# Four moves in the order of an encoder block's kernel: an earlier load for the second MLP operand, weight blocks that join later, two spacings changed

## The chip, the cores and the metric

The kernel runs on one core of a Trainium2 chip. The metric is the device time of one execution in microseconds, lower is better, as the median of several executions.

## The reference

One layer of a bidirectional encoder, for 1024 tokens of width 1024 in float32:

```
u = rms_norm(x);  q,k,v,cB,cC,cH,gA,gB = split(u @ w_in)
y_A = neighbourhood_attention(rms_norm(q), rms_norm(k), v) @ w_attn_branch
y_B = (cB * conv3(cC * cH)) @ w_conv_branch
m   = sigmoid(gA) * y_A + sigmoid(gB) * y_B
x   = x + m @ w_o
x   = x + relu(rms_norm(x) @ w_mlp_in)^2 @ w_mlp_out
```

The MLP's inner width is 4096.

## The kernel before, in words

The engines are named as in the profile: PE (TensorE, matmuls), DVE (VectorE), ACT (ScalarE), POOL (GpSimd) and SP (SyncE, whose queue issues every load, store and DMA transpose). Each engine works through its own instructions in the order in which the program issued them; an instruction that waits holds up all that stand behind it on its engine.

**Numbers.** Every float32 operand is scaled by a power of two and split into two float16 parts, high and low (ACT makes the high part by a scaled copy, DVE the low part by a multiply and subtract). A product is three passes over those parts (high by high, high by low, low by high). The scale of a weight block needs the block's largest value or sum of squares over all partitions. DVE reduces along each partition (L301 and L309 for a `Chunk`, L924 for the `forms_sum` blocks), writes a column (`ones_col`, L311 or L925), and PE adds it up with a 128 x 128 matmul of ones (`all_sum`, L179). These one-column matmuls stand in PE's stream like any other product.

**Seven products for eight.** The gates (S), the MLP's first product (W1) and its second (W2) are made with a 2 x 2 block scheme that needs seven block products. Its inputs are sums and differences of blocks ("forms"); its outputs are put together from the seven products by DVE. For a gate group or a W1 group `seven` issues seven units of twelve matmuls; each unit takes a PSUM bank in turn (`anybank`, eight banks under the names d, s and o).

**What orders the work.** The instructions' order is set when the program is built, by a hand-written schedule. `unit` issues the matmuls of one unit, then calls `step` and `tick` a given number of times. `step` advances every generator of the list `fg` (work that follows from products), `tick` advances the first generator of the list `bg` (preparation of later weights). A generator that yields is continued at a later tick. `apart` makes a generator wait until so many units, or so many matmul columns (`work`), have been issued. `built` and `need` drive the background list by force until a block is ready. `load_upto` issues the next weight loads on SP when an earlier block has been split and its buffer is free (five `raw` buffers in turn).

**Stages around the change.**
- *Gate groups*, n = 0 to 7. At the start of group n the preparation of S for n+1 (`prep_s`) is put on the background list, and for n = 1, 3, 5 that of the next A and B blocks (the projections of the attention and convolution branches, `Chunk.prep`). Then the group's products (`gate_units`), then those with A and B (`branch_units`), which `built` makes wait for the blocks. `turn_s` issues DMA transposes of the activations on SP.
- *Output projection* (`proj`, lines 1217 to 1248): 16 units of 24 matmuls with the blocks O0 and O1. O1's preparation is put on the background list ahead of them. After the units of the second half, `pair(n)` normalises two row blocks, makes the forms (L1138), splits them (L1163 on ACT, L1165 on DVE) and issues two DMA transposes (L1169) into u2T and u2x, the activations of the MLP's first product. `pair` makes a form only when the transposes of the pair before it have been issued, and issues those only when W1's group 0 is ready.
- *MLP, first product*: 16 groups q (`quad`), each with its W1 block (`sums1`, `prep1`). DVE's posts (L1295, L1298, L1299, L1300, L1303, L1308, L1310) put the products together and free their banks; `h_done` then squares (L1269, L1271), adds on POOL (L1138) and stores the forms of h to DRAM (L1275). Each store holds four groups' parts of one quarter s.
- *MLP, second product*: 28 operands, seven for each quarter, numbered 16 to 43. `prep2` makes one: ACT and DVE split the h form (L1384, L1386), then the weight (L1389, L1393). Its buffer becomes free when the products of group or operand i-2 are issued (`gate`). Operand 16 uses w11, 17 the form t2, made by POOL (L1399, L1400) after operand 16's splits. The load of h for operand 16 is issued by `first2`, for operand 17 inside the loop (L1377), for 18 and on by `h_load` (L1343).

Of the kernel before, what the change touches and what calls it, by code (L numbers as in the profile page):

```python
# [10 lines left out]
F32 = mybir.dt.float32  # L11
F16 = mybir.dt.float16
# [40 lines left out]
def encoder_block(ctx: ExitStack, tc: tile.TileContext, x, weights, cols, gqk, rel, masks, out):  # L53
# [106 lines left out]
    def apart(mark, n=3, of=units):  # L160
        while of[0] < mark + n and not forced[0]:
            yield WAIT
# [57 lines left out]
    class Chunk:  # L220
# [75 lines left out]
        def largest(self, rm, a, b):  # L296
            o = 0
            for p, (k, w) in enumerate(self.widths):
                while len(self.raw) <= p:
                    yield WAIT  # L300
                V.tensor_reduce(sc[:, at(rm, o, k)], self.raw[p][:, :k * w].rearrange("p (k w) -> p k w", k=k),  # L301
                                axis=AX, op=OP.max, apply_absolute_value=True)
                o += k
                yield
            while not self.ready:
                yield WAIT
            mul(rm, self.rows, rm)
            yield
            V.tensor_reduce(sc[:, a], sc[:, rm], axis=AX, op=OP.max, apply_absolute_value=True)  # L309
            c = ones_col()  # L310
            V.tensor_copy(c, sc[:, a])  # L311
            if self.kind != "V":
                yield from apart(units[0], {"A": 3, "B": 3, "O": 1}[self.kind])
            yield from all_sum(c, b, bank(self.bank) if self.bank else anybank(), 1e-30, self.kind != "V")

    def push(*chunks):
        for ch in chunks:
            bg.append(ch.prep())
# [602 lines left out]
    def sum_of(sm):  # L921

        b, a = cols_of("prep", 1), ones_col()
        V.tensor_reduce(sc[:, b], sc[:, sm], axis=AX, op=OP.add)  # L924
        V.tensor_copy(a, sc[:, b])  # L925
        return a, work[0]
# [136 lines left out]
    for n in range(8):  # L1063
        built(cG if n == 0 else cS[n])
        if n < 7:
            bg.append(prep_s(n + 1))
        if n in (1, 3, 5):
            push(cA[n // 2 + 1], cB[n // 2 + 1])
        m = w3p.tile([128, 2, 512], F32, name="m", bufs=1)
        mf = m.rearrange("p a t -> p (a t)")  # L1070
        if n < 7:
            sg = gate_units(n)
            if n == 0:
                turn_s(0, 2)

            def post(g, half, ps, iv, sg=sg, m=m):
                t = sg[:, 2 * half + g]
                V.scalar_tensor_tensor(t, ps, iv, t, op0=OP.mult, op1=OP.mult)
                if g == 1:
                    V.tensor_tensor(m[:, half], sg[:, 2 * half], t, op=OP.add)  # L1080
            branch_units(n, post)
            late.append(lambda n=n, mf=mf: fg.append(m_done(n, mf)))
        else:
            push(cO[0])
            tick(4)
            y = w3p.tile([128, 4, 512], F32, name="gsum", bufs=1)
            branch_units(n, lambda g, half, ps, iv: A.activation(y[:, 2 * half + g], ps, AF.Copy, scale=iv))
            settle()
            drain()
            s7 = tmp()  # L1090

            def bound():
                mm, m2, mx = tmp(4), tmp(2), tmp()
                V.tensor_reduce(sc[:, mm], y, axis=AX, op=OP.max, apply_absolute_value=True)
                yield
                V.tensor_tensor(sc[:, m2], sc[:, mm.start:mm.start + 4:2], sc[:, mm.start + 1:mm.start + 4:2],
                                op=OP.add)
                V.tensor_reduce(sc[:, mx], sc[:, m2], axis=AX, op=OP.max)
                yield from pow2(mx, 14, s7, at(rowsM, 7))
                for ch in cO:  # L1100
                    ch.ready = True

            fg.append(bound())

            def last(sg, half):
                o = slice(2 * half, 2 * half + 2)
                V.tensor_tensor(sg[:, o], sg[:, o], y[:, o], op=OP.mult)
                V.tensor_tensor(m[:, half], sg[:, 2 * half], sg[:, 2 * half + 1], op=OP.add)
                t = slice(512 * half, 512 * half + 512)
                A.activation(M[0][:, 7, t], m[:, half], AF.Copy, scale=sc[:, s7])  # L1110
                V.scalar_tensor_tensor(M[1][:, 7, t], m[:, half], sc[:, s7], M[0][:, 7, t],
                                       op0=OP.mult, op1=OP.subtract)

            gate_units(7, last)
            X1 = base.tile([128, 8, D], F32, name="x1", tag="Q")
            for b in range(8):
                SP.dma_start(X1[:, b], x[b * 128:(b + 1) * 128, :])
            settle()
# [73 lines left out]
    def sums1(q):  # L1192

        ch = c1[q]
        while q == 2 and pair_done[0] < 4:
            yield
        if q == 0:
            tsum[0] = U2[1][:, 2].rearrange("p s k t -> p (s k t)").bitcast(F32).rearrange("p (i c) -> p i c", i=4)
        elif q % 2:
            t = wsp.tile([128, 2, 4, 512], F32, name="tsum", tag="ws")  # L1200
            for i in range(2):
                tsum[q + i] = t[:, i]
        yield from rows_scaled(ch, g2)
        yield from forms_sum(ch, tsum[q], 3 if q > 1 else 2)

    def prep1(q):

# [13 lines left out]
    def proj(b, half, post=None, mms=None):  # L1221
        ps = anybank()

        def fin():
            o = X1[:, b, 512 * half:512 * half + 512]
            V.scalar_tensor_tensor(o, ps, sc[:, cO[half].inv], o, op0=OP.mult, op1=OP.add)
            if post:
                post()
        mm = tok_mms(ps, actM, b, cO[half], 8, 512, 0)
        if mms is None:  # L1230
            unit(mm, fin, 6, 4)
        else:
            mms.append((mm, fin))

# [112 lines left out]
    def prep2(s):  # L1347
# [11 lines left out]
        for i in range(2):  # L1359
            A.activation(j, x2[:, 2 * i:2 * i + 2].rearrange("p a c -> p (a c)"), AF.Square, scale=sc[:, iR],  # L1360
                         accum_out=sc[:, at(sm, 4 + i)])
            yield
        sw, inv = yield from scale_of(sum_of(sm), 0)
        fw = keep()
        mul(iR, sw, fw)
        c2[s].inv = inv
# [2 lines left out]
        for o, (f, name) in enumerate(ORDER):  # L1369
            n = 7 * s + o  # L1370
            i = 16 + n
            yield from gate(i)
            pool, tag = TAGS[i % 3]
            P = OPS[i] = pool.tile([128, 2, 2, 2048], F16, name="ops", tag=tag)
            if n == 1:
                later["h", 1] = P[:, 0].rearrange("p w m -> p (w m)").bitcast(F32).rearrange("p (k t) -> p k t", k=4)
                SP.dma_start(later["h", 1], HS[0][:, ORDER[1][0]])  # L1377
                yield from wait(8)
            while ("h", n) not in later:
                yield  # L1380
            if 1 < n < 26:
                h_load(n + 2)
            hf = later.pop(("h", n)).rearrange("p k t -> p (k t)")
            A.activation(P[:, 1, 0], hf, AF.Copy, scale=sc[:, Rs])  # L1384
            yield
            V.scalar_tensor_tensor(P[:, 1, 1], hf, sc[:, Rs], P[:, 1, 0], op0=OP.mult, op1=OP.subtract)  # L1386
            w = {"w11": w11, "t1": w11, "t3": w12, "w21": w21, "w22": w22}.get(name) or [T2[:, i] for i in range(2)]
            for i2 in range(2):
                A.activation(P[:, 0, 0, 1024 * i2:1024 * i2 + 1024], w[i2], AF.Copy, scale=sc[:, fw])  # L1389
            yield  # L1390
            for i2 in range(2):
                sl = slice(1024 * i2, 1024 * i2 + 1024)
                V.scalar_tensor_tensor(P[:, 0, 1, sl], w[i2], sc[:, fw], P[:, 0, 0, sl], op0=OP.mult, op1=OP.subtract)  # L1393
                yield
            ready.add(i)
            if name == "w11":
                T2 = later["t2"]()
                for i2 in range(2):
                    G.tensor_tensor(w11[i2], w11[i2], w12[i2], op=OP.add)  # L1399
                    G.tensor_tensor(T2[:, i2], w11[i2], w22[i2], op=OP.add)  # L1400
                    yield
            elif name == "t2":
                for i2 in range(2):
                    G.tensor_tensor(w12[i2], w12[i2], w22[i2], op=OP.add)
                yield
            elif name == "t3":
                for i2 in range(2):
                    G.tensor_tensor(T2[:, i2], T2[:, i2], w21[i2], op=OP.add)
                yield
            elif name == "t1":  # L1410
                done[0] += 4
                load_upto(done[0] + 5)
                if s < 3:
                    w2x_load(s + 1)
                    bg.append(prep2(s + 1))
            yield
# [146 lines left out]
```

## Time and profile before

| | |
|---|---|
| median of 3 runs | 1305.25 us (1305.03 to 1309.44) |
| the profiled execution | 1304.02 us, of which the span 1302.2 |
| mean granted TensorE clock in it | 0.979 |
| PE busy | 1220.6 us, 6294 matmuls |
| DVE busy | 933.8 us, 1719 instructions |
| ACT busy | 763.3 us, 1169 |
| POOL busy | 436.5 us, 269 |
| DMA | 173.35 MB, mean 133 GB/s |

Times in the text are microseconds from the start of the span of this execution. In a line of the timeline the columns are start, duration, engine, line, operation, output<-input and shape, and how many alike follow each other; in brackets stands the idle time of the engine before it and what ended it. A window's line gives its length, the busy time of PE, PEld, DVE, ACT and POOL with their counts, then the granted clock, the DMA share and GB/s. Ends of matmuls are modelled: a 128x512 matmul has 0.38 as its own, while one starts every 0.216 at full clock.

### The profile page before, as it was taken

How to read it: one execution, taken by the hardware profiler on the slowest of the kernel's cores; microseconds unless marked ns; L12 is line 12 of the kernel's file. 1: busy time of each engine (PE TensorE's matmuls, PEld its weight loads, DVE VectorE, ACT ScalarE, POOL GpSimd, SP SyncE). 2: the span in 40 equal slices, each digit the busy share in tenths (PEclk: the TensorE clock that was granted, in tenths of full speed). 3: DMA queues.
4: the chain of work that ended last, by engine and by line, in shares of the span. 5: the costliest groups of instructions: out<-in, count | busy, mean ns of one | idle time of the engine just before them, and what ended most of it. 6: DMA issues, size and time to landing. Idle time of an engine off the chain costs nothing.

```text
span 1302.2 us, 17008 instructions
## 1 busy us (share of the span) xinstructions
PE 1220.6 (94%) x6294; PEld 580.2 (45%) x6294; DVE 933.8 (72%) x1719; ACT 763.3 (59%) x1169; POOL 436.5 (34%) x269
## 2 busy tenths in 40 slices
PE   4999998888998999999997899999997799999998
PEld 3444444444443444444456444444443344444443
DVE  6578767878648776776575476667744588889798
ACT  6777567667454444524665678777773564646530
POOL 2430010121220211101022576667735516080562
PEclk9999998999999999999998999999998899999999
DMA  6558435646552121325284443445453662626112
GB/s 249 125 194 160 108 68 122 131 89 130 118 117 87 48 65 33 84 65 208 53 163 109 146 168 133 160 162 178 161 203 121 221 255 83 241 98 242 65 65 97
DMA packets 170803, 173.35 MB, mean 133 GB/s; under 512 B 131424, under 2 KB 131936, under 8 KB 166624
## 3 DMA queue, kind: packets, MB, share of 16 engines
q1 hardware_dynamic: 170720, 172.27, 44.8%
q8 instruction: 49, 0.80, 0.2%
q14 instruction: 34, 0.28, 0.1%
HBM read 102.51 MB, written 37.75 MB: 108 GB/s over the span
## 4 chain that ended last, share of the span: by engine, by line
PE 61%; DVE 13%; issue 8%; ACT 7%; DMA 7%; POOL 4%; SPq 1%; DVEq 0%; POOLq 0%; ACTq 0%
PE ps_d L188 22%; PE ps_s L188 19%; PE ps_o L188 13%; PE ps_d L854 4%; DVE w_ws L278 1%; DMA PT<-P 1%; DMA u2x<-v 1%; POOL as L1138 1%; DMA xt<-in_x 1%; DVE ops L1393 1%; DVE P L818 1%; DVE sz L792 1%; ACT w L977 1%; POOL sform L480 1%; DMA hf<-hs 1%
## 5 line engine op out<-in xcount | busy, mean ns | idle before, releaser
L188 PEld LDWEIGHTS <-w 128*128 128x128 f16 x1512 | 149.4, 100 | 160.4 <-issue 9.4
L188 PEld LDWEIGHTS <-ops 128*128 128x128 f16 x1356 | 133.1, 98 | 182.7 <-issue 21.2
L1138 POOL TENSOR_TENSOR as<-as 128x512 f32<-128x512 f32 x64 | 111.7, 1745 | 95.2 <-ACT as L1271 91.4
L188 PE MATMUL ps_s<-ops 128*128 128x512 f16 (+1 forms) x528 | 123.1, 384 | 17.6 <-ACT ops L1389 7.0
L854 PE MATMUL ps_d<-uT,w_ws 128*128 128x512 f16 x528 | 129.1, 386 | 2.4 <-ACT w_ws L290 2.4
L188 PE MATMUL ps_d<-ops 128*128 128x512 f16 x492 | 112.9, 379 | 0.0
L188 PEld LDWEIGHTS <-uT 128*128 128x128 f16 x648 | 64.4, 100 | 70.4 <-issue 6.8
L1384 ACT ACTIVATE ops<-hf,sc 128x2048 f16<-128x2048 f32 x26 | 51.9, 1994 | 70.4 <-PE ps_d L188 24.6
L188 PE MATMUL ps_d<-u2T,w 128*128 128x512 f16 (+1 forms) x420 | 90.1, 367 | 3.2 <-DMA u2T<-v 2.8
L188 PEld LDWEIGHTS <-w_s 128*128 128x128 f16 x588 | 57.0, 98 | 74.5 <-issue 6.1
L971 DVE SCALAR_TENSOR_TENSOR w<-raw,sc,w 128x512 f16<-128x512 f32 (+1 forms) x32 | 40.7, 1270 | 67.3 <-ACT w L977 67.3
L188 PE MATMUL ps_s<-u2x,w 128*128 128x512 f16 (+1 forms) x396 | 84.5, 364 | 2.1 <-DMA u2x<-v 2.0
L1386 DVE SCALAR_TENSOR_TENSOR ops<-hf,sc,ops 128x2048 f16<-128x2048 f32 x26 | 70.7, 2717 | 16.1 <-ACT ops L1384 16.1
L188 PE MATMUL ps_o<-ops 128*128 128x512 f16 x336 | 77.7, 379 | 2.1 <-DVE ops L1393 1.5
L958 POOL TENSOR_TENSOR tsum<-raw 128x512 f32<-128x512 f32 x30 | 50.6, 1702 | 85.2 <-ACT raw L944 69.7
L944 ACT ACTIVATE raw<-raw,sc 128x256 f32<-128x256 f32 x184 | 75.9, 494 | 4.7 <-DMA raw<-in_weights 4.7
L854 PEld LDWEIGHTS <-w_ws 128*128 128x128 f16 x528 | 51.3, 99 | 59.1 <-issue 5.2
L1399 POOL TENSOR_TENSOR raw<-raw 128x1024 f32<-128x1024 f32 x8 | 22.7, 2837 | 136.1 <-DVE ops L1393 136.1
L958 POOL TENSOR_TENSOR gsum<-raw 128x512 f32<-128x512 f32 x14 | 19.8, 1418 | 140.7 <-ACT raw L944 125.6
L1269 ACT ACTIVATE as<-as 128x2048 f32<-128x2048 f32 x16 | 30.6, 1910 | 60.5 <-DVE as L1303 60.5
L971 DVE SCALAR_TENSOR_TENSOR w<-tsum,sc,w 128x1024 f16<-128x1024 f32 x30 | 61.4, 2087 | 0.0
L278 DVE SCALAR_TENSOR_TENSOR w_ws<-raw,sc,w_ws 128x512 f16<-128x512 f32 (+2 forms) x72 | 51.2, 765 | 3.5 <-ACT w_ws L290 3.5
(300 smaller groups left out, 2525.1 us busy)
## 6 DMA issues: line engine op xcount, KB each, us to landing
raw<-in_weights SPq DMA_DIRECT2D x92, 512.0 KB, 4.0
hs<-as SPq DMA_DIRECT2D x16, 1792.0 KB, 6.9
hf<-hs SPq DMA_DIRECT2D x26, 1024.0 KB, 10.9
w2x<-in_weights SPq DMA_DIRECT2D x16, 512.0 KB, 7.0
raw<-in_weights SPq DMA_DIRECT2D x16, 384.0 KB, 3.8
xt<-in_x SPq DMA_DIRECT2D x8, 512.0 KB, 9.8
gs<-s SPq DMA_DIRECT2D x4, 1024.0 KB, 6.8
x<-in_x SPq DMA_DIRECT2D x8, 512.0 KB, 8.7
```

The lines of the kernel that those rows point to most:

```text
L188: T.matmul(ps, l, r, start=a, stop=b)
L278: V.scalar_tensor_tensor(lo, self.raw[p][:, o:o + m], sc[:, c:c + 1], hi, op0=OP.mult, op1=OP.subtract)
L480: G.tensor_tensor(f[:, o], a, b, op=op)
L854: T.matmul(ps, l, r, start=a, stop=b)
L944: A.activation(v, v, AF.Copy, scale=sc[:, at(g, 4 * i + k)])
L958: G.tensor_tensor(t[:, o], a, b, op=OP.add)
L971: V.scalar_tensor_tensor(P[:, a:b, 1], w, sc[:, s], P[:, a:b, 0], op0=OP.mult, op1=OP.subtract)
L1138: sub.tensor_tensor(z[o], z[a], z[b], op=op)
L1269: A.activation(f[:, 0:4], f[:, 0:4], AF.Relu)
L1384: A.activation(P[:, 1, 0], hf, AF.Copy, scale=sc[:, Rs])
L1386: V.scalar_tensor_tensor(P[:, 1, 1], hf, sc[:, Rs], P[:, 1, 0], op0=OP.mult, op1=OP.subtract)
L1399: G.tensor_tensor(w11[i2], w11[i2], w12[i2], op=OP.add)
```

## The change

It makes four moves; no arithmetic, load or matmul is added or taken away.
1. For n = 1, 3, 5 the A and B blocks are put on the background list after the gate group's seven products, not before.
2. The ones matmul of O1 waits for two units in place of one. (A, B and O0 stay as they were.)
3. In `forms_sum` the gap ahead of the ones matmul of W1's group 1 is one in place of two (group 0's stays two); and the units of the second half of the output projection for row blocks 2, 3, 6 and 7 are followed by six ticks in place of four.
4. The load of operand 17's h is issued in `prep2` before the scale of the weights, as soon as group 14's products are issued; in the loop the load and eight yields behind it are gone.

```diff
             if self.kind != "V":
-                yield from apart(units[0], {"A": 3, "B": 3, "O": 1}[self.kind])
+                yield from apart(units[0], 3 if self.kind != "O" else 1 + (self is cO[1]))
...
-        if n in (1, 3, 5):
-            push(cA[n // 2 + 1], cB[n // 2 + 1])
         m = w3p.tile([128, 2, 512], F32, name="m", bufs=1)
         mf = m.rearrange("p a t -> p (a t)")
         if n < 7:
             sg = gate_units(n)
+            if n in (1, 3, 5):
+                push(cA[n // 2 + 1], cB[n // 2 + 1])
...
-        yield from forms_sum(ch, tsum[q], 3 if q > 1 else 2)
+        yield from forms_sum(ch, tsum[q], 3 if q > 1 else 2 - q)
...
-            unit(mm, fin, 6, 4)
+            unit(mm, fin, 6, 4 + 2 * (half and b % 4 > 1))
...
-        sw, inv = yield from scale_of(sum_of(sm), 0)
+        sums = sum_of(sm)
+        if s == 0:
+            yield from gate(17)
+            P = OPS[17] = TAGS[17 % 3][0].tile([128, 2, 2, 2048], F16, name="ops", tag=TAGS[17 % 3][1])
+            later["h", 1] = P[:, 0].rearrange("p w m -> p (w m)").bitcast(F32).rearrange("p (k t) -> p k t", k=4)
+            SP.dma_start(later["h", 1], HS[0][:, ORDER[1][0]])
+        sw, inv = yield from scale_of(sums, 0)
...
-            P = OPS[i] = pool.tile([128, 2, 2, 2048], F16, name="ops", tag=tag)
-            if n == 1:
-                later["h", 1] = P[:, 0].rearrange("p w m -> p (w m)").bitcast(F32).rearrange("p (k t) -> p k t", k=4)
-                SP.dma_start(later["h", 1], HS[0][:, ORDER[1][0]])
-                yield from wait(8)
+            if n != 1:
+                OPS[i] = pool.tile([128, 2, 2, 2048], F16, name="ops", tag=tag)
+            P = OPS[i]
```

## The prediction

> **What bounds the kernel now.** I read the page first: busy times, the granted clock, the chain that ended last.
>
> ```profile
> PE 1220.6 (94%) x6294; PEld 580.2 (45%) x6294; DVE 933.8 (72%) x1719; ACT 763.3 (59%) x1169; POOL 436.5 (34%) x269
> PEclk9999998999999999999998999999998899999999
> PE 61%; DVE 13%; issue 8%; ACT 7%; DMA 7%; POOL 4%; SPq 1%; DVEq 0%; POOLq 0%; ACTq 0%
> ```
>
> TensorE is busy for 1220.6 of 1302.2 us, and the change leaves its 6294 matmuls as they are. So only its 82 idle us can be won, and the low clock behind idle stretches. I looked these up in the timeline of each engine, by place. First, the gate group of n = 1 (SP, DVE, PE, then a window after it):
>
> ```profile
> 377.22 10.36 SPq L916 DMA_TRANSPOSE uT<-gs  x8
> 387.68 1.47 SPq L210 DMA_DIRECT2D raw<-in_weights  x3
> 393.32 1.22 DVE L301 TENSOR_REDUCE sc<-raw 128x4 f32<-128x1024 f32 x1 [8.96 <-DMA raw<-in_weights]
> 395.30 0.16 PE L179 MATMUL ps_d<-ones 128*128 128x1 bf16 x1 [3.67 <-DVE ones L311]
> 395.32 4.44 PE L188 MATMUL ps_s<-qD,w_s 128*128 128x512 f16 x12
> 395.80:399.10 3.30, 3.30 (x9) 1.17 (x8) 3.23 (x7) 0.00 (x0) 0.00 (x0) 0.50 0.00 0
> ```
>
> A1's load stands on SP behind eight transposes; DVE waits 8.96 for it, the ones matmul 3.67 for DVE. Behind that the clock is 0.50 for 3.3 us: twelve matmuls take 4.44 where twelve elsewhere take 2.75. The place costs 3.67 + 1.69 = 5.4.
>
> Second, O1's ones matmul, and the turning of the activations for W1 (PE, SP):
>
> ```profile
> 601.61 0.16 PE L179 MATMUL ps_d<-ones 128*128 128x1 bf16 x1 [2.12 <-DVE ones L311]
> 644.96 6.26 SPq L1169 DMA_TRANSPOSE u2T<-v  x1
> 658.25 4.86 SPq L1169 DMA_TRANSPOSE u2T<-v  x1
> 663.20 3.61 SPq L1169 DMA_TRANSPOSE u2x<-v  x1
> 670.62 1.47 PE L188 MATMUL ps_s<-u2x,w 128*128 128x256 f16 x12
> 698.30 1.61 PE L188 MATMUL ps_d<-u2T,w 128*128 128x256 f16 x12 [2.84 <-DMA u2T<-v]
> ```
>
> Wait at 601: no half clock behind it (matmuls follow at 0.216). At 670.62 PE starts 0.13 after the transpose landed (670.49): no slack. At 698.30 it waits for the last pair's transposes.
>
> Third, the start of the second MLP product (ACT, DVE, POOL, PE):
>
> ```profile
> 994.94 2.00 ACT L1384 ACTIVATE ops<-ops,sc 128x2048 f16<-128x2048 f32 x1 [14.88 <-DMA ops<-hs]
> 980.02 4.50 DVE L1393 SCALAR_TENSOR_TENSOR ops<-raw,sc,ops 128x1024 f16<-128x1024 f32 x2
> 1000.61 2.48 DVE L1393 SCALAR_TENSOR_TENSOR ops<-h,sc,ops 128x1024 f16<-128x1024 f32 x2 [1.28 <-ACT ops L1389]
> 1003.00 0.68 DVE L1303 TENSOR_TENSOR as<-ps_s,as 128x512 f32<-128x512 f32 x1
> 991.53 2.35 POOL L1400 TENSOR_TENSOR h<-raw,w2x 128x1024 f32<-128x1024 f32 x1
> 1000.62 0.58 PE L188 MATMUL ps_s<-ops 128*128 128x512 f16 x1 [7.05 <-ACT ops L1389]
> 1032.94 0.59 PE L188 MATMUL ps_s<-ops 128*128 128x512 f16 x1 [6.86 <-ACT acc L1483]
> ```
>
> The second operand's h comes late (ACT idle 14.88), and PE waits 7.05. But its weights T2 come from POOL, whose last sum ends at 993.88. The fourth operand's stall (6.86) hangs on L1303 at 1003.00, from which L1269, L1271, four L1138, the store and the load of h follow.
>
> All sums are against the profiled execution, 1304.02 us (span 1302.2 and 1.8 around it); the median of the runs is 1305.25, so I add the differences to that.
>
> **A and B blocks behind the gate products.** No instruction is added; two times four reduces (L301, 1.22) with their small operations join after the seven products, for n = 1, 3, 5. For n = 1 they then stand behind S2's splits, over 10 us after the loads land at 393.3 to 396. DVE's wait and PE's go: -5.4. What had been hidden behind that wait? uT itself lands at 389.0, ahead of it: nothing new there. Price: S3's splits now run behind A1's and B1's scales and splits (sixteen operations, 0.4 to 0.5 each). Before, the last split of S3 (L971) ends at 440.36 and its reader starts at 443.70: 3.3 of slack. With PE 5.4 earlier the reader is due at 438.3; were the split to stay it would cost 2.1, and following the rows from the unit that releases its sums it ends near 438. S5 is alike. Taken 0, ends 0 and +2.1. Term: -5.4, ends -5.6 and -3.3.
>
> **O1's sums one unit later.** The ones matmul passes one unit of 24 matmuls, 24 x 0.216 = 5.2: PE reaches it at 604.5, the column is there at 601.55. The 2.12 go (2.3 with the restart). But all behind it on the background list follows a unit later: O1's splits (still in time: last needed some 4.7 us after the first), the W1 loads that these release, and W1 group 0's sum and splits. And pair(0)'s transposes wait until group 0 is ready, pair(1)'s forms until pair(0)'s are issued; that PE has no slack for. On PE's clock: before, group 0's second L971 ends at 644.47, SP's second load behind it, and u2T starts at 644.96. After, the unit ahead ends at 643.3; L1226 and L410 0.9, L977 0.70, L971 0.75, L977 and L971 to 647.3: 2.8 late. The next pair's L1158 now stand among eight L944 (0.40 apart), so its L1165 ends at 662.5 in place of 658.22: 4.3 late. Then 4.86 and 3.61 on SP and 1.9 to 3.7 to land: 672.9 to 674.8, against PE's 670.6. PE gets a new wait of 2.3 to 4.2, in place of the waits of 0.55 and 1.24 at 680 to 682 and part of those to 702. What lasts is how late the last pair's transposes come, since they are what PE waits for at the end of this stage: between 2 and 4.3, I take 3.0. Term: -2.3 + 3.0 = +0.7, ends -2.3 (no lag lasts) and +2.0.
>
> **Group 1's sums, and two ticks more.** Its ones matmul moves 24 matmuls ahead (position 3383 for 3407), its four splits ahead of one L1307. They were what PE waited for at 680.50 and 682.13 (1.79), but the transposes come after and cover it: 0. If that cover is gone, -1.8. The two extra ticks pull background steps ahead, in the same order. Group 0's gap stays 2.
>
> **The second operand's load.** It moves on SP from behind the store at 983.46 to where group 14's last products free its buffer, 963.6; in its new place SP has nothing waiting behind it before that store. Loads land in issue order (four of h at 1028.2 to 1035.6, 2.5 apart), so it lands behind the store of 959.26 (landed 972.43), at about 975, before ACT is done with the first operand (980): free. Shared evenly it would hold that store back by up to 2.5, and with it ACT's next step: this is in the +0.5 below only in part, and in the third rival. The eight yields are gone too, so its preparation is issued ahead of group 15's L1298, L1299, L1300, L1303 on DVE. Now L1393's second half waits for T2 (POOL, 993.88) with L1298 to L1303 queued behind it, and those free the PSUM banks that the first operand's fourth unit (L1298) and the second's first, third and fourth need (L1299, L1300, L1303). So PE stalls one unit earlier, from 990.82. By the rows: L1389 1.13 after 993.88, L1393 1.28 (POOL idle, 1000.61) or 2.29 (POOL at work, 980.02), L1298 0.68: 997.0 to 998.0; POOL's L1399 takes 2.35 alone and 3.34 beside DVE, up to 1.0 more: 999.0. After POOL's sums for T2 come its L1404, so I take the slow rows: 998.6. Two units (5.2) and the half clock as before (3.4) then bring the second unit of the second operand to 1007.2, about where it starts today (1006.59). L1303 ends at 998.6 + 3 x 0.68 = 1000.6 in place of 1003.69: the hs store, h's load and the fourth operand come 3.0 earlier. The 1.1 at the third operand (0.75 and clock, 1017.07) goes, hidden in that. Term: -3.0, ends -4.9 (fast rows) and +0.5.
> A rule of the Trainium skill speaks against this part: GPSIMD Engine Reference, "1. Specifications", says that its SBUF interfaces are shared with VectorE, in contention with DVE instructions that have two SBUF inputs. L1393 has two, and the trace agrees (2.29 against 1.28); L1298, with one from PSUM, takes 0.68 beside POOL. By the rule the term is -3.0; were there no such contention it would be -4.9.
>
> **Sum.** -5.4 + 0.7 + 0 - 3.0 = -7.7: 1296.3 profiled, 1305.25 - 7.7 = 1297.5 in the runs.
>
> **Rivals.**
> The whole of both MLP stalls goes: 5.4 + 2.3 + 10.6 (993 to 1006 with its clock) + 9.5 (1026 to 1038) = 28: 1277. For it: the load lands 20 us earlier. Against: T2 at 993.88 and DVE's order. 0.06.
> Nothing is given back at the transposes and POOL runs undisturbed: -5.4 - 2.3 - 4.9 = -12.6: 1292.7, spread 1291 to 1295. For it: the lag is a chain of eight links, each could be covered. 0.22.
> Most is given back: lag 4.3, S3 and S5 late by 2.1 and 1, the MLP 0 : -5.4 - 2.3 + 4.3 + 3.1 = -0.3, down to -5: 1300 to 1305. 0.15.
> Slower: pair(1) falls back a second unit, because its forms queue behind the W1 scales on ACT. Lag 3.0 + 5.2 = 8.2, and two half-clock windows (2 x 1.7) for a stall that long: -5.4 - 2.3 + 8.2 + 3.4 - 3.0 = +0.9, 1306, up to 1313 if pair(2) does likewise. It decides from a lag of 10.7 on, clock included. Against: in the changed order the forms follow one unit later only. 0.10.
> The change does nothing: the wait at 395 only gives way to another, the rest is hidden: 1305. Against: uT has landed. 0.02.
> My forecast, with clock windows of 1.7 either way: 1295 to 1300, 0.45.
>
> **From cases to numbers.** 1291 to 1304 holds forecast, second and most of the third rival. Within 0.5% (6.5 us, about what a measurement of this kernel tells from no change) means above 1298.7. Faster: 0.29 of the forecast, 0.22, 0.06: 0.57. Same: 0.16, 0.15, 0.04, 0.02: 0.37. Slower: 0.06.
>
> **What would show it.** At 391 PE runs on, clock 1.0; the ones matmul at 601 doesn't wait. A new wait of 2 to 4 us on u2x or u2T at the first W1 products, and none on L977. PE's wait of 7 to 8 us stands one unit earlier, released by L1298, and DVE's idle time before L1393 ends with ACT's L1389 on POOL's sum; the fourth operand's wait is still over 4 us. Wrong: no wait at the first W1 products (1293), or PE not waiting at the MLP's start (1277).

## The result, and the profile after

The changed kernel takes 1297.41 us (median of 5 runs, 1294.54 to 1298.12) beside 1305.03 for the kernel before (5 runs): a ratio of 0.9935, interval 0.9914 to 0.9957. The forecast was 1297.5. The profiled execution took 1298.12, 5.9 less than that of before; its span is 1296.0, 6.2 less. From line 1363 on, line numbers in kernel.py have moved: L1384, L1386, L1389, L1393, L1399, L1400 and L1483 of before are L1388, L1390, L1393, L1397, L1403, L1404 and L1487 now.

The page after: the busy times stay, the granted clock's row has five eights in place of four, the last three of them where they were.

```profile
PE 1217.8 (94%) x6294; PEld 579.5 (45%) x6294; DVE 940.0 (73%) x1719; ACT 763.9 (59%) x1169; POOL 433.7 (33%) x269
PEclk8999999989999999999998999999998899999999
```

PE's timeline after, at the places that the prediction took up: gate group 1, the first W1 products, and the end of the turning.

```profile
389.68 2.55 PE L188 MATMUL ps_s<-uT,w_s 128*128 128x512 f16 x11 [0.85 <-DMA uT<-gs]
392.06 2.75 PE L188 MATMUL ps_d<-qD,w_s 128*128 128x512 f16 x12
394.65 0.17 PE L179 MATMUL ps_s<-ones 128*128 128x1 bf16 x1
...
666.08 2.12 PE L188 MATMUL ps_s<-u2x,w 128*128 128x256 f16 x12 [2.09 <-DMA u2x<-v]
683.88 2.72 PE L188 MATMUL ps_o<-u2T,w 128*128 128x256 f16 x12 [3.96 <-DVE as L1298]
693.78 2.53 PE L188 MATMUL ps_d<-u2T,w 128*128 128x256 f16 x12 [2.89 <-DMA u2T<-v]
```

At 394.65 the ones matmul follows without a wait, and at O1's the timeline has no idle time any more. In their place stands 2.09 on u2x, which before had no wait; the two waits at 680 to 682 are gone, and the wait for L1298 behind them is 3.96 in place of 2.02.

PE, DVE and POOL at the start of the second MLP product, after:

```profile
995.48 5.28 PE L188 MATMUL ps_d<-ops 128*128 128x512 f16 x12 [9.72 <-DVE as L1298]
1025.94 0.59 PE L188 MATMUL ps_s<-ops 128*128 128x512 f16 x1 [4.16 <-ACT acc L1487]
```

```profile
979.21 4.43 DVE L1390 SCALAR_TENSOR_TENSOR ops<-ops,sc 128x2048 f16<-128x2048 f32 x1
987.07 2.17 DVE L1397 SCALAR_TENSOR_TENSOR ops<-h,sc,ops 128x1024 f16<-128x1024 f32 x1 [2.83 <-ACT ops L1393]
992.65 2.17 DVE L1397 SCALAR_TENSOR_TENSOR ops<-h,sc,ops 128x1024 f16<-128x1024 f32 x1 [3.41 <-ACT ops L1393]
994.75 0.68 DVE L1298 TENSOR_TENSOR as<-ps_d,as 128x512 f32<-128x512 f32 x1
996.66 0.68 DVE L1303 TENSOR_TENSOR as<-ps_s,as 128x512 f32<-128x512 f32 x1
...
978.17 3.33 POOL L1403 TENSOR_TENSOR raw<-raw 128x1024 f32<-128x1024 f32 x1
981.57 4.28 POOL L1404 TENSOR_TENSOR h<-raw,w2x 128x1024 f32<-128x1024 f32 x1
...
988.24 3.20 POOL L1404 TENSOR_TENSOR h<-raw,w2x 128x1024 f32<-128x1024 f32 x1
```

PE waits 9.72 for L1298, one unit earlier than before; L1298 stands behind two L1397, each of which waits through ACT for POOL. The load is not what is waited for: it landed at 970.37, and ACT's L1388 reads it at 974.73. A new thing is the pair 979.21 and 981.57: L1390 on DVE takes 4.43 (2.35 before) and L1404 on POOL 4.28 (2.34 before). The rows show them taking turns: L1390 starts while POOL's L1403 runs and ends 2.15 after it; L1404 starts while L1390 runs and ends 2.21 after that.

How far PE is ahead of the kernel before, by place, from the starts of the same matmuls in the two traces (each number is the change across that stretch; negative means that PE gains there):

| stretch | after | forecast |
|---|---|---|
| gate group 1 (uT's last matmuls to the next group) | -4.2 (-5.3 from the ones matmul on, +1.1 at uT) | -5.4 |
| O1's ones matmul | -2.3 | -2.3 |
| from there to the last pair's transposes | +2.1 | +3.0 |
| the two MLP waits, with their clock | -1.0 | -3.0 |

With 0.5 us for what came before the change's first place and about 0.3 elsewhere this is -6.2 at the last matmul.

### The profile page after: what moved, and what is told of

Same layout as the page of the kernel before. It is cut to its first block, busy times and chain, and to the rows that moved or that the text cites. A ratio compares the mean times of both kernels' runs of the same rounds, so it can differ in the third digit from the quotient of the medians.

```text
span 1296.0 us, 17018 instructions
## 1 busy us (share of the span) xinstructions
PE 1217.8 (94%) x6294; PEld 579.5 (45%) x6294; DVE 940.0 (73%) x1719; ACT 763.9 (59%) x1169; POOL 433.7 (33%) x269
## 5 line engine op out<-in xcount | busy, mean ns | idle before, releaser
L1138 POOL TENSOR_TENSOR as<-as 128x512 f32<-128x512 f32 x64 | 111.7, 1746 | 85.3 <-ACT as L1271 81.6
L1388 ACT ACTIVATE ops<-hf,sc 128x2048 f16<-128x2048 f32 x26 | 51.8, 1994 | 69.7 <-PE ps_d L188 24.7
L1390 DVE SCALAR_TENSOR_TENSOR ops<-hf,sc,ops 128x2048 f16<-128x2048 f32 x26 | 70.7, 2718 | 16.0 <-ACT ops L1388 16.0
L1403 POOL TENSOR_TENSOR raw<-raw 128x1024 f32<-128x1024 f32 x8 | 22.7, 2837 | 140.8 <-DVE ops L1397 140.8
```

What stands on the lines that cost most here:

```text
L1138: sub.tensor_tensor(z[o], z[a], z[b], op=op)
```

## The experiments

The theory was the sum of the prediction: the blocks give all of the gain but 2 to 3 us, O1's spacing is given back at the transposes, W1's sums do nothing, the load turns the second operand's wait into one for L1298. The main rivals: each move keeps its gain, and the load ends the MLP waits. In the diffs, "-" is the kernel named first.

**e1, the blocks alone.** Kernel before, one part of the change.

```diff
-        if n in (1, 3, 5):
-            push(cA[n // 2 + 1], cB[n // 2 + 1])
...
             sg = gate_units(n)
+            if n in (1, 3, 5):
+                push(cA[n // 2 + 1], cB[n // 2 + 1])
```

> Before, with the A and B blocks put on the list behind the gate products, and nothing else. My theory: the wait of 3.67 at 391 and the half clock behind it go, 5.4 us, and nothing takes their place: median near 1299.6. Rival: what was hidden behind the wait (the transposes of uT, S3's splits) comes out, the gain is under 2 us.

Measured: 1299.84 beside 1304.05, ratio 0.997 (0.9952 to 0.9988). Its trace, PE at the same place:

```profile
388.67 2.55 PE L188 MATMUL ps_s<-uT,w_s 128*128 128x512 f16 x11 [0.32 <-DMA uT<-gs]
391.05 2.75 PE L188 MATMUL ps_d<-qD,w_s 128*128 128x512 f16 x12
393.64 0.17 PE L179 MATMUL ps_s<-ones 128*128 128x1 bf16 x1
```

PE gains 4.9 across this stretch. S3's and S5's late splits show as two waits of 0.14 and 0.10 (0.3 each with the restart), at 438 and 495. The theory holds, and the rival's 2 us are outside what the trace shows; the runs alone (gain 1.6 to 6.3) would not tell 2 from 4.

**e2, O1's spacing alone.** Kernel before.

```diff
-                yield from apart(units[0], {"A": 3, "B": 3, "O": 1}[self.kind])
+                yield from apart(units[0], 3 if self.kind != "O" else 1 + (self is cO[1]))
```

> Before, with O1's ones matmul one unit later, and nothing else. My theory: PE gains 2.1 to 2.3 at 599 to 601 and gives it back at the first W1 products, where it now waits 2 to 4 us for u2x: from the last transposes on it is 0 to 1.5 us later than before. Rival: no new wait on u2x, 2.3 us gained to the end.

Measured: 1303.12 beside 1304.05, ratio 0.9994 (0.9979 to 1.0009). PE in its trace:

```profile
669.58 2.45 PE L188 MATMUL ps_s<-u2x,w 128*128 128x256 f16 x12 [2.06 <-ACT v L1163]
```

PE passes O1's ones matmul 2.3 earlier, waits 2.06 for u2x, and takes up the last pair's transposes 0.4 later than before, counted from its entry into this stage. What follows behind that place differs by the clock (below). The trace bears the theory out; the runs (a gain of -1.2 to 2.7) would not exclude the rival's 2.3 by themselves.

**e3, the load alone.** Kernel before, with the last two hunks of the change.

> Before, with the load of the second operand's h begun behind group 14, and nothing else. My theory: PE's wait stands one unit earlier and is longer (8 to 10 us, released by L1298), the fourth operand's wait is shorter, together 1 to 3 us gained. Rival: the early load ends the waits, 10 to 20 us gained.

Measured: 1301.99 beside 1304.05, ratio 0.999 (0.9975 to 1.0005).

```profile
1001.67 5.28 PE L188 MATMUL ps_d<-ops 128*128 128x512 f16 x12 [9.71 <-DVE as L1298]
1031.44 0.57 PE L188 MATMUL ps_s<-ops 128*128 128x512 f16 x1 [3.39 <-ACT acc L1487]
```

The wait for L1298 is 9.71, as in the changed kernel to 0.01; the fourth operand's is 3.39 in place of 6.86. Over both PE gains 3.0 here, 1.0 in the changed kernel and 0.3 in e4, with the same order of instructions. In all three the load of the fourth operand's h is issued 27.19 after the start of the first operand's third unit (28.31 before), so the order of the work gives 1.1. The rest lies in that load, which lands 10.3 after its issue here, 11.0 in the changed kernel, 12.0 in e4 and 11.7 before, and in the half clock behind the wait, which costs 1.0 less here than in the other two. The rival's 10 to 20 us are out.

**e4, the change without O1's spacing.**

```diff
-                yield from apart(units[0], 3 if self.kind != "O" else 1 + (self is cO[1]))
+                yield from apart(units[0], {"A": 3, "B": 3, "O": 1}[self.kind])
```

> The changed kernel, with O1's spacing as before (one unit). My theory: the wait of 2.1 at 599 is back, the wait of 2.1 on u2x at the first W1 products is gone; the median is within 1.5 us of the changed kernel's. Rival: the spacing is worth its 2.3 us, the median is 2 to 3 us above the changed kernel's.

Measured: 1295.43, ratio to before 0.9936 (0.9915 to 0.9957); the changed kernel has 0.9935 (0.9914 to 0.9957). The wait of 2.12 at O1's ones matmul is back, that on u2x is gone. By medians it is 2.0 faster, half a microsecond more than expected; by the ratios there is no difference. Each interval reaches 2.7 us to either side, so the runs alone would not exclude the rival (2 to 3 slower). The trace speaks against it: from O1's place to the last pair's transposes PE gains 0.7 here and 0.2 in the changed kernel.

**e5, POOL without its neighbour.** The changed kernel; it leaves out the low part of operand 17's h, and ACT writes a copy in its place.

```diff
-            V.scalar_tensor_tensor(P[:, 1, 1], hf, sc[:, Rs], P[:, 1, 0], op0=OP.mult, op1=OP.subtract)
+            if n == 1:
+                A.activation(P[:, 1, 1], hf, AF.Copy, scale=sc[:, Rs])
+            else:
+                V.scalar_tensor_tensor(P[:, 1, 1], hf, sc[:, Rs], P[:, 1, 0], op0=OP.mult, op1=OP.subtract)
```

> The changed kernel, with the low part of the second operand's h (one L1390 on DVE, 128x2048, beside POOL) left out: ACT writes a copy there. Theory contention: POOL's L1404 beside it, 4.28 us in the changed kernel, takes 2.3, L1298 comes 1.5 to 2.5 us earlier after the first operand's last L1397, PE's wait of 9.7 shrinks to 7.2 to 8.2. Rival, POOL's own pace: L1404 stays above 4 us and PE's wait above 9.

One run, 1294.49. POOL and PE (L1407 and L1298 are the changed kernel's L1404 and L1298):

```profile
980.65 2.34 POOL L1407 TENSOR_TENSOR h<-raw,w2x 128x1024 f32<-128x1024 f32 x1
992.61 5.28 PE L188 MATMUL ps_d<-ops 128*128 128x512 f16 x12 [7.78 <-DVE as L1298]
```

POOL's sum takes 2.34 in place of 4.28, PE's wait falls by 1.94, the whole of it. So POOL's sum had waited for DVE's split, and that alone put the wait 1.9 above the 7 to 8 of the prediction. The load of the fourth operand's h is now issued 25.26 after the start of the first operand's third unit, 3.05 earlier than before: the 3.0 that the prediction had.

**e6, eight yields back.** The changed kernel, the load left early.

```diff
             P = OPS[i]
+            if n == 1:
+                yield from wait(8)
             while ("h", n) not in later:
```

> The changed kernel, with the eight yields put back ahead of the second operand's splits (the load stays early). Theory head of line: L1298, L1299, L1300 go ahead of the L1397 that waits for POOL, PE's wait moves back to the second operand's first unit and is 3 to 5 us shorter than before's 7.8, the fourth operand's wait stays over 4; 4 to 7 us gained on the changed kernel, median 1291 to 1293.5. Rival: PE waits for POOL's sum all the same, within 1.5 us of the changed kernel.

Measured: 1295.48, ratio to before 0.993 (0.9915 to 0.9945). In e6 and e7 the lines behind the insertion have moved by two: L1390, L1393, L1397, L1403 and L1404 of the changed kernel are L1392, L1395, L1399, L1405 and L1406.

```profile
990.05 1.24 PE L188 MATMUL ps_s<-ops 128*128 128x512 f16 x5 [0.87 <-DVE ops L1399]
993.43 0.38 PE L188 MATMUL ps_s<-ops 128*128 128x512 f16 x1 [2.14 <-ACT ops L1395]
994.75 2.12 PE L188 MATMUL ps_s<-ops 128*128 128x512 f16 x5 [0.94 <-DVE ops L1399]
1023.98 0.58 PE L188 MATMUL ps_s<-ops 128*128 128x512 f16 x1 [6.29 <-ACT acc L1489]
```

The wait moves to the second operand's first unit and is 3.95 in three pieces, against 7.79 before and 9.72 in the changed kernel: the part on the order is shown. But the fourth operand's wait is 6.29 again, since L1303 still goes behind the second L1399 that waits for POOL. PE gains 4.0 over both waits (1.0 in the changed kernel), and the median is 1.9 under the changed kernel's, 0.7 by the ratios: less than the 4 to 7 expected, as part of the gain at the one is paid back at the other.

This trace also shows who waits for whom on POOL and DVE:

```profile
982.20 2.35 POOL L1406 TENSOR_TENSOR h<-raw,w2x 128x1024 f32<-128x1024 f32 x1
984.51 4.41 POOL L1405 TENSOR_TENSOR raw<-raw 128x1024 f32<-128x1024 f32 x1
...
982.35 4.35 DVE L1392 SCALAR_TENSOR_TENSOR ops<-ops,sc 128x2048 f16<-128x2048 f32 x1
```

L1406 started 0.15 ahead of DVE's split and is not slowed; the split is, and then the sum that starts behind it.

**e7, twelve yields.** The same with wait(12).

> The changed kernel, with twelve yields there: L1303 too goes ahead of the second operand's splits, and the hs store, the load of h behind it and the fourth operand follow it. Theory: the fourth operand's wait (4.5) goes as well, the median is 8 to 12 us under the changed kernel's, 1285.5 to 1289.5. Rival: POOL does the four L1138 of the last group ahead of or between the sums for T2, the second operand comes later by 4 to 8 us and the median is within 3 us of that with eight yields.

Measured: 1283.68 beside 1304.48, ratio 0.9844 (0.9828 to 0.986).

```profile
979.63 0.68 DVE L1303 TENSOR_TENSOR as<-ps_s,as 128x512 f32<-128x512 f32 x1
986.31 2.44 DVE L1392 SCALAR_TENSOR_TENSOR ops<-ops,sc 128x2048 f16<-128x2048 f32 x1 [1.36 <-ACT ops L1390]
...
990.05 0.59 PE L188 MATMUL ps_s<-ops 128*128 128x512 f16 x1 [3.79 <-ACT ops L1395]
992.36 4.26 PE L188 MATMUL ps_s<-ops 128*128 128x512 f16 x11 [1.73 <-DVE ops L1399]
```

L1303 now comes at 979.63 (996.66 in the changed kernel); the store of the last forms goes out at 995.67 (1009.62), and the fourth operand has no wait at all. The second operand's is 5.52. Over both places PE gains 13.5 on before, 4.0 of it up to the third operand and 9.4 at the fourth. This and e9 are the best kernels of the study: 13.7 under the changed one by medians, 11.9 by the ratios, where 8 to 12 were expected. The rival is out: POOL does the four L1138 behind the sums for T2, not ahead of or between them. What twelve yields would give with the load as late as before was not tried; the 9.4 hang on L1303's place, so they may not need the early load.

**e8, W1's sums alone.** Kernel before.

```diff
-        yield from forms_sum(ch, tsum[q], 3 if q > 1 else 2)
+        yield from forms_sum(ch, tsum[q], 3 if q > 1 else 2 - q)
...
-            unit(mm, fin, 6, 4)
+            unit(mm, fin, 6, 4 + 2 * (half and b % 4 > 1))
```

> Before, with only the spacing of W1's group 1 and the two extra ticks. Theory: it moves group 1's sum ahead but the last pair's transposes still end the stage: within 1.5 us of before. Rival: the waits of 0.55 and 1.24 at 680 to 682 go and stay gone, 1.8 us or more gained.

Measured: 1301.63 beside 1304.48, ratio 0.9982 (0.9972 to 0.9992): a gain of 1.0 to 3.7. The theory's 1.5 is missed by the median. In the trace the last pair's transposes come 0.6 earlier, counted from PE's position behind O1's wait and the half clock that follows it; the wait of 0.55 is gone, that of 1.24 is 0.99. 0.6 is all that the order of the work gives. Most of the rest in this trace is the clock: before has four slow stretches of 3.41 us between 682 and 707, this kernel two. But e1, which has before's spacing, has two there as well, so that this move causes it is not shown. This trace also shows what O1's wait can cost (PE, and a window behind it):

```profile
600.35 0.16 PE L179 MATMUL ps_d<-ones 128*128 128x1 bf16 x1 [2.13 <-DVE ones L311]
```

```profile
601.80:605.00 3.20, 3.20 (x9) 1.06 (x7) 0.52 (x4) 2.52 (x5) 0.00 (x0) 0.50 0.01 3
```

The wait is 2.13 as in before, but here the half clock follows it, 1.7 more.

**e9, twelve yields without O1's spacing** (e7 with the edit of e4).

> The kernel with twelve yields, with O1's spacing as before (one unit). Theory: the 2.1 us at O1's ones matmul come back and the 2.1 us on u2x go: median within 1.5 us of the kernel with twelve yields (1283.7). Rival: with the rest changed the spacing is worth 2 us or more one way or the other.

Measured: 1283.98 beside 1305.16, ratio 0.9845 (0.9826 to 0.9864), 0.3 above e7. As expected, the runs show no worth of the spacing here.

**e10, u2T's transposes set free.** e7, and in `pair`:

```diff
-            while 0 not in ready:
+            while a and 0 not in ready:
                 yield
```

> The kernel with twelve yields, and pair's transposes into u2T no longer wait for W1's group 0 (those into u2x still do). Theory: the lag of O1's spacing is the wait of the pairs for group 0; SP starts 2 to 5 us earlier, the wait of 2.1 on u2x shrinks by half or more, and 0.5 to 2 us of O1's 2.3 are kept: median 1281.5 to 1283.5. Rival: the lag is in ACT's and DVE's order, not in SP's; the wait on u2x stays at 2 and the median within 0.5 us of 1283.7.

Measured: 1284.87 beside 1305.16, ratio 0.9852 (0.9839 to 0.9866).

```profile
634.90 4.81 SPq L1169 DMA_TRANSPOSE u2T<-v  x1
645.05 4.81 SPq L1169 DMA_TRANSPOSE u2x<-v  x1
655.82 4.85 SPq L1169 DMA_TRANSPOSE u2T<-v  x1
660.76 3.63 SPq L1169 DMA_TRANSPOSE u2x<-v  x1
```

Counted from O1's place, the first pair's transposes go out 6.6 and 3.0 earlier than in e7, the second pair's at the same time to 0.1, and the wait on u2x is 2.09 (2.05 in e7). So the lag that PE meets is not in SP's hold on u2T, and the theory is out. The rival has the wait right but not the median, which is 1.2 above e7's in place of within 0.5, with intervals that overlap. That the lag is in ACT's and DVE's order is not shown: the second pair's forms still wait until the first's u2x transpose is issued, and that for group 0; lifting this was not tried.

## Why the prediction was right, point by point

**The blocks: right, in size a little large.** -5.4 against -4.9 in e1 and -5.3 from the ones matmul on in the changed kernel. The price of S3's and S5's splits, taken 0 with an end of +2.1, is 0.3 each. The 5.4 are also what one execution had to lose there: in e2 and e8, with before's order, PE gets the last of uT 2.2 and 1.4 later, the ones matmul waits 0.51 and 1.66 in place of 3.67, and no half clock follows. From the unit ahead of uT's last matmuls to the first matmuls on s4T, PE gains 4.3 more in the kernels with the new order than in those with the old, on average over eight traces and four.

**O1's spacing: right in kind, a little large in size.** The 2.3 go as forecast. The lag of the transposes behind PE's own gain is in e2 3.9 at the second pair (forecast 4.3), 2.8 at the third, 2.7 at the last (forecast 3.0): net +0.4 in place of +0.7. The kernels with W1's sums agree: up to the last pair PE gains 0.7 without the spacing (e4; e9, counted behind its half clock) and 0.0 to 0.2 with it (the changed kernel, e5, e6, e7, e10). The new wait is 2.09 in the changed kernel, 0.2 under the 2.3 to 4.2 of the text. What it left out: O1's wait is followed by a stretch at half clock, which costs 1.7, in some executions (e8, e9) and not in others (before, e1, e3, e4), and the new wait on u2x likewise (1.7 in e2, the changed kernel, e6 and e10, none in e5 and e7). I had counted the restart only.

**W1's sums: the term 0 was short.** The place shows -0.6 in e8 (-0.7 in e4 and e9), e8's runs -1.0 to -3.7. The step that failed is "the transposes come after and cover it": they come 0.6 earlier themselves. With O1's +0.4 this makes -0.2 at the last pair in the changed kernel, which is what its trace has.

**The load: right in mechanism, a term mis-sized.** The load landed at 970.37 (the forecast's 975 is 969.8 on this kernel's clock, where PE is 5.2 ahead), the wait moved one unit ahead and released by L1298, L1393 behind POOL's sum, the fourth operand's wait still over 4: all there. But I let L1393 and one L1399 pay for POOL and DVE at work together, up to 1.0, and not the longest instruction: the second operand's L1386 (now L1390), which starts during POOL's first sum, so that the second sum waits for it and takes 4.28 for 2.34. T2 came 2.8 later than by the rows of before, PE's wait was 9.72 and not 7 to 8, and the term -1.0 in place of -3.0 (-0.3 to -3.0 in three traces of this order, of which the order of the work gives -1.1 in each). e5 puts 1.94 on this one pair, the difference between -1.1 and -3.0. The end of -4.9 for the fast rows is itself 0.2 too large: by 997.0 L1303 would end at 999.0, 4.7 ahead of 1003.69. The rule of the Trainium skill that was weighed beside it (GPSIMD Engine Reference, "1. Specifications") spoke the right way, and the trace agrees; the price, 1.94 for one pair, was larger than the 1.0 of the rows of before.

**The sum.** -7.7 forecast, -7.6 by medians, -5.9 in the profiled pair. The errors (+0.5 at the blocks by e1, -0.9 at O1 and W1's sums, +2.0 at the load) cancel in part and leave +1.6, about what the profiled pair shows. The half clock moves single executions by about as much: so the agreement of the medians to 0.1 is luck, that within 2 is not. The rival in which both MLP waits go (28 in all) was wrong for this change. With the same load and another order on DVE, e7 comes to 21, with the second operand's wait still 5.5.

## What to carry to other kernels

A load brought forward frees only the wait on that load; before it is credited with the stall, look up what else the consumer reads, and what stands behind the consumer on its own engine: here four posts that free PE's banks stood behind a split that waited for POOL, and issuing them first as well was worth about 12 us, the early load by itself 0 to 3. When a wait is taken from the list that prepares everything later, count the lag that the list hands on, to the place where the chain has no slack, and cost it net.

Where two engines are seen to wait for each other's instructions, cost the longest instruction that the new order sets beside the chain, not the pair that the old trace happened to show.

## What the runs showed of the hardware

DVE's splits and POOL's sums, which have no operand in PSUM, take turns by whole instructions. In the changed kernel L1390 (2.35 alone) starts at 979.21, 2.29 before POOL's L1403 ends, and ends 2.15 after it; L1404 (2.34 alone) starts at 981.57, during L1390, and ends 2.21 after that. The one that started first is not slowed: in e6 L1406 keeps its 2.35 although DVE's split starts 0.15 behind it, and the split takes 4.35. DVE's posts, with one operand from PSUM, keep their 0.68 beside POOL.

A wait of PE of 2.1 us is followed by a stretch at half clock in some executions and not in others: at O1's ones matmul in e8 and e9, not in before, e1, e3 and e4, at the same length to 0.01. The slow stretches in one trace begin whole multiples of 3.41 us apart (in the one of before at 395.7, 682.5, 689.3, 699.5, 743.9 and 996.5, among others). Cut into steps of 3.41 on that grid, the traces show what decides: in e8 and e9 the wait lies in one step but for at most 0.06, in which PE is busy for 0.39 and 0.38, and the next step is slow; in the other four it falls across two steps, each busy for 0.55 or more, and none is slow. Over all twelve traces, behind a step at full clock with PE busy for under 0.4 of it, the next is at 0.50 in all 80 cases; between 0.4 and 0.5 in 8 of 51; above 0.5 in none of some 4100. (From 40 us on; two steps that reach past the last matmul are left out; busy by the rows, whose ends are modelled.)
